# Modulation sums moved to the tensor engine, and the first expert's tokens chosen by rank

## The chip, the core and the metric

The kernel runs on one core of one Trainium2 chip. The metric is the device time of one execution in microseconds; shown is the median over runs. A profile is one further execution, recorded by the hardware profiler. All numbers in the model are float32.

## The reference, cut to what matters

The kernel computes a mixture-of-experts block followed by two layers of another block (feed-forward, mixer, feed-forward). Only the first block is touched by the change:

```python
SEQ = 256; D_MODEL = 1024; N_EXPERTS = 16; EC_CAPACITY_FACTOR = 2; D_FF_EXPERT = 2048

def expert_choice_moe(h, w_router, w_gate, w_up, w_down):
    cap = EC_CAPACITY_FACTOR * S // E                                  # 32 tokens
    affinity = jax.nn.softmax((h @ w_router).astype(jnp.float32), axis=-1)
    gates, idx = lax.top_k(jnp.swapaxes(affinity, 1, 2), cap)          # each expert picks its tokens
    xe = h[b_idx, flat_idx].reshape(B, E, cap, D)
    a = jnp.einsum('becd,edf->becf', xe, w_gate)
    u = jnp.einsum('becd,edf->becf', xe, w_up)
    ye = jnp.einsum('becf,efd->becd', jax.nn.silu(a) * u, w_down)
    ye = ye * gates[..., None].astype(ye.dtype)
    return jnp.zeros_like(h).at[b_idx, flat_idx].add(ye.reshape(B, E * cap, D).astype(h.dtype))

# first_block
mod = jax.nn.silu(c) @ w_ada[l] + b_ada[l]
shift_m, scale_m, gate_m, shift_f, scale_f, gate_f = [m[:, None, :] for m in jnp.split(mod, 6, axis=-1)]
h = rmsnorm(x, g_pre_mix[l]) * (1.0 + scale_m) + shift_m
proj = h @ w_in[l]
...                                       # retention and dilated attention, y_ret and y_att
mixed = jnp.concatenate([y_ret, y_att], axis=-1) @ w_out[l]
x = x + gate_m * rmsnorm(mixed, g_post_mix[l])
h = rmsnorm(x, g_pre_ffn[l]) * (1.0 + scale_f) + shift_f
moe = expert_choice_moe(h, w_router[l], w_gate_e[l], w_up_e[l], w_down_e[l])
x = x + gate_f * rmsnorm(moe, g_post_ffn[l])
```

The six modulations are numbered j = 0 to 5 below. The three weight matrices of one expert have 8 MiB each; the sixteen experts together have 384 MiB.

## The kernel before, in words

Tokens lie on the partitions in two tiles of 128 (t = 0, 1); the model width of 1024 is cut into eight pieces of 128 (k). Large products are made from a rounded high part and a remainder: `pieces` splits a weight on ScalarE (high) and on VectorE or GpSimd (remainder), and `mm3` (L115 to L117) does three matmuls.

The first block is the function `first`. Modulations 0 and 1 are computed at once: `mod_bank` (L253) multiplies a weight by `cb`, the vector silu(c) copied 32 times, so that each matmul fills 32 of the 128 PSUM rows (L260). Then a loop of 16 steps runs: `chan` computes 128 columns of the in-projection (24 matmuls of 128x258; its small side products are L474), then `mod_step(i)` does a part of modulations 2 to 5, then a piece of attention or retention. On every second step `mod_step` loads 512 rows of `w_ada` (2 MiB, `ada` and `block`), and on each step `mod_unit` adds two rows of eight into an accumulator `macc` on VectorE (L308 for the first, L310 for the rest, 128x1024 each). A modulation that is ready is summed over the partitions on TensorE, with `macc` as the weights (`mod_sum_cols`, L316) or a matrix of ones (`mod_sum_rows`, L329).

Behind the loop stand the out-projection (`mmo`), the residual (`to_x`, L348 and L350, with the tile `yg`, whose upper half is `gm`), the router's logits (transposes L728, copies L730 and L732, matmuls L735, softmax L737 to L741), and the choice of tokens: the affinities are transposed (L742), four rounds of max and replace find 32 tokens for each of the 16 experts (L780, L781), a running sum gives each its place (L782 to L785), and the places become one-hot matrices `sall` (L797). The tokens of expert 0 are gathered with `xh` and `xl`, the high and low parts of the scaled `x` (L806 and L807, four matmuls for each of the eight pieces k), into `x0`; the others' are gathered into `xe` between the two down blocks of expert 0.

`experts` (L872) goes through the experts in order. Each has two blocks of gate and up weights (4 MiB each, matmuls L898), then silu, a product (L911), four transposes, and two blocks of down weights (L943). A block of 4 MiB lies in a tile of the pool `ringx`, which has three (`xblock`, L91). Expert 0 also uses tiles left free by the stages before: four of `ring` for its second gate block (`unit`, L65), and nine `wx` tiles for its first down block (`extra`, L706).

All weight loads are issued by SyncE's queue, one after the other. A load waits there until the last reader of its tile is done, and everything behind it in the queue waits too. Instructions on each engine run in the order of the program as a list scheduler writes it.

Of the kernel before, what the change touches and what calls it, by code (L numbers as in the profile page):

```python
# [15 lines left out]
P = 128  # L16
# [19 lines left out]
class K:  # L36
# [3 lines left out]
    def __init__(s, ctx, tc):  # L40
# [5 lines left out]
        s.nblock = s.npiece = 0  # L46
# [167 lines left out]
    def consts(s):  # L214
# [13 lines left out]
        V.tensor_tensor(s.dist, s.r1, s.r2, OP.add)  # L228
        n = s.tmp()
# [68 lines left out]
    def mod_row(s, I, i, acc, eng):  # L298

        s.nc.gpsimd.memset(acc, 0.0)  # L300
        eng.dma_start(acc[0:1, :], I["b_ada"][0:1, i * D:(i + 1) * D])
# [10 lines left out]
    def mod_sum_cols(s, i, acc):  # L312

        pt = s.bank("acc", (KT, 2))
        for k in range(KT):
            s.nc.tensor.matmul(pt[:, k, :], s.quads(acc, k), s.one[:, :2], start=True, stop=True)  # L316
        mc = s.sm.tile([P, 2, 4], F32, tag="mc", name="mc", bufs=4)
        s.nc.vector.tensor_tensor(mc, s.fcol[:, 2 + 2 * i:4 + 2 * i, :], pt.rearrange("p (q r) o -> p q r o", r=4)[:, :, :, 0], OP.add)
        return mc
# [5 lines left out]
    def mod_sum_rows(s, acc, out):  # L325

        for n in range(2):
            pt = s.bank("acc")
            s.nc.tensor.matmul(pt, s.one, acc[:, half(n)], start=True, stop=True)  # L329
# [33 lines left out]
    def first(s, I, mid):  # L363
# [21 lines left out]
        V.memset(one, 1.0)  # L385

# [75 lines left out]
        shb = sm.tile([P, KT, 32], F32, name="shb", bufs=1, tag="cb")  # L462
# [140 lines left out]
        def mod_step(i):  # L603
            j, u = 2 + i // 4, i % 4
            if u == 0:
                accm[j] = t4("av", (D,)) if j == 5 else pa.tile([P, D], F32, tag="xn", name="macc", bufs=2)
                if j == 2:
                    s.mod_row(I, j, accm[j], A)
            if u % 2 == 0:
                accm["w"] = s.ada(I, j, u // 2)  # L610
            s.mod_unit(accm["w"][u % 2], u, accm[j], j > 2)
# [80 lines left out]
        ex0 = []  # L692

        def next_dma(d):

            if s.last0:
                s.queue(d, s.last0)
            s.last0 = d

        s.last0 = None  # L700

        def extra(*tiles):
            for pool, tag, m, n in tiles:
                u = pool.tile([P, m], F32, tag=tag, name="wx", bufs=n)
                o = sum(i.shape[1] for i in ex0)
                s.udma = nc.sync.dma_start(u, s.rows_x(I, "w_down_e", 0, 0)[:, o:o + m])  # L706
                next_dma(s.udma)
                ex0.append(u)

        t1 = lambda tag: (pa, tag, 1024, 1)  # L710
        extra(*[t1(i) for i in ("aq", "ak", "rqk", "rv")])
# [5 lines left out]
        pa_t = s.bank("tr")  # L717
# [5 lines left out]
        def logits(t):  # L723
# [18 lines left out]
            T.transpose(pa_t[:ne, tok(t)], aff[:, t, :], s.ident)  # L742
# [6 lines left out]
        s.ringx = s.c1.enter_context(s.tc.tile_pool(name="ringx", bufs=3, reuse_waits="tile"))  # L749
        w0 = {}  # L750
        for b in range(2):
            for n in ("w_gate_e", "w_up_e"):
                v = s.rows_x(I, n, 0, b)
                if b and n == "w_gate_e":
# [821 lines left out]
```

## Time and profile before

| what | us |
|---|---|
| median of three runs (2278.76 to 2280.75) | 2280.57 |
| the profiled execution's own time | 2279.83 |
| its span in the profile | 2278.1 |
| PE busy in the span | 1869.2 |
| VectorE busy in the span | 984.5 |
| ScalarE busy in the span | 730.3 |

The program has four parts on the time line: the start and the in-projection loop to about 153 us, the out-projection and the router to about 199 us, the sixteen experts to about 1111 us, and the second block behind them. PE is the tensor engine, PEld its weight loads, DVE VectorE, ACT ScalarE, POOL GpSimd, SP SyncE; an engine's name with a q is its queue of DMA issues. A matmul of float32 appears as two instructions in the trace, so counts there are twice those in the code. A matmul's time in the trace runs to its modelled end, so that neighbours overlap: the distance between two starts is what each costs. PEclk is the granted share of the tensor engine's full clock, 2.4 GHz; at 0.5 it runs at 1.2 GHz.

### The profile page before, as it was taken

The page shows a single profiled execution, that of the slowest core. Times are in us where ns is not written, and L with a number is a line of the kernel's source. Part 1 is how long each engine was busy: PE and PEld are TensorE (multiplying, and loading weights), DVE is VectorE, ACT ScalarE, POOL GpSimd, SP SyncE. Part 2 cuts the span into 40 slices and gives each one's busy share as a digit, 9 for nine tenths or more (in the row PEclk, how much of TensorE's full clock was granted, in tenths as well). Part 3 has the DMA queues.
Part 4 walks back from the last instruction along what each step waited for, and adds up shares of the span by engine and source line. Part 5 has one row for each costly group of instructions (what it writes and reads, how often), then busy time and mean ns, then how long its engine had stood idle before and what let it go on. Part 6 is the DMA issues. An engine that isn't in the chain of part 4 may idle for free.

```text
span 2278.1 us, 29561 instructions
## 1 busy us (share of the span) xinstructions
PE 1869.2 (82%) x12453; PEld 1352.3 (59%) x12453; DVE 984.5 (43%) x1577; ACT 730.3 (32%) x1205; POOL 157.1 (7%) x164
## 2 busy tenths in 40 slices
PE   7898765565555566556699999999999999999998
PEld 5685211111111111111399989899999998989997
DVE  6984200000000010000365568965556556896554
ACT  4542000000000000000254456854435445685443
POOL 2321000000000000000100032200000003200000
PEclk9997888878788778888799999999999999999999
DMA  8857999999999999999865545546546555544651
GB/s 329 328 222 329 435 432 429 430 429 432 429 429 431 432 429 431 431 432 430 311 231 182 199 166 181 181 157 222 186 156 222 181 198 166 176 171 164 220 185 56
DMA packets 190547, 659.58 MB, mean 290 GB/s; under 512 B 6867, under 2 KB 144331, under 8 KB 177486
## 3 DMA queue, kind: packets, MB, share of 16 engines
q1 hardware_dynamic: 189452, 657.06, 74.1%
q8 instruction: 97, 1.59, 0.3%
q10 hardware_dynamic: 962, 0.64, 0.1%
q14 instruction: 36, 0.29, 0.0%
HBM read 656.62 MB, written 1.05 MB: 289 GB/s over the span
## 4 chain that ended last, share of the span: by engine, by line
PE 59%; DMA 30%; DVE 5%; ACT 2%; POOL 2%; issue 1%; ACTq 0%; SPq 0%; POOLq 0%; DVEq 0%
DMA w<-in_w_down_e_dram 15%; DMA w<-in_w_gate_e_dram 14%; PE up L115 8%; PE up L117 8%; PE up L116 8%; PE acc L116 6%; PE acc L117 6%; PE acc L115 5%; PE acc L898 4%; PE up L943 4%; PE up L150 4%; PE up L154 2%; POOL uc L1255 1%; DVE v L1286 1%; DMA w<-in_w_up_e_dram 1%
## 5 line engine op out<-in xcount | busy, mean ns | idle before, releaser
L102 DVE TENSOR_TENSOR hl<-w,hl 128x1024 fp32r<-128x1024 f32 x376 | 458.0, 1230 | 253.7 <-ACT hl L101 253.5
L101 ACT ACTIVATE hl<-w 128x1024 fp32r<-128x1024 f32 x388 | 404.8, 1057 | 271.6 <-PE up L117 106.4
L115 PE MATMUL up<-hTh,hl 128*128 128x256 f32 x1664 | 470.2, 283 | 1.1 <-ACT uc L1276 1.1
L116 PE MATMUL up<-hTl,hl 128*128 128x256 f32 x1664 | 467.4, 281 | 0.0
L117 PE MATMUL up<-hTh,hl 128*128 128x256 f32 x1664 | 467.4, 281 | 0.0
L115 PEld LDWEIGHTS up<-hTh,hl 128*128 128x128 f32 x1664 | 313.3, 188 | 4.1 <-ACT uc L1276 1.9
L116 PEld LDWEIGHTS up<-hTl,hl 128*128 128x128 f32 x1664 | 313.6, 188 | 1.9
L117 PEld LDWEIGHTS up<-hTh,hl 128*128 128x128 f32 x1664 | 313.5, 188 | 0.0
L943 PE MATMUL up<-w,tmp 128*32 128x512 f32 x992 | 155.1, 777 | 104.7 <-DMA w<-in_w_down_e_dram 104.2
L900 ACT ACTIVATE tmp<-acc 128x512 f32<-128x512 f32 x16 | 9.6, 597 | 700.3 <-PE acc L898 700.3
L911 DVE TENSOR_TENSOR tmp<-tmp,acc 128x512 f32<-128x512 f32 x16 | 11.0, 688 | 514.7 <-PE acc L898 514.7
L115 PE MATMUL acc<-hl,a 128*128 128x512 f32 x528 | 209.9, 398 | 0.0
L116 PE MATMUL acc<-hl,a 128*128 128x512 f32 x528 | 208.6, 395 | 0.0
L117 PE MATMUL acc<-hl,e 128*128 128x512 f32 x528 | 208.6, 395 | 0.0
L898 PE MATMUL acc<-w,rqk 128*32 128x512 f32 x480 | 96.3, 944 | 126.7 <-DMA w<-in_w_up_e_dram 66.3
L943 PEld LDWEIGHTS up<-w,tmp 128*32 128x32 f32 x992 | 38.7, 137 | 209.4 <-issue 112.9
L898 PE MATMUL acc<-w,aq 128*32 128x512 f32 x480 | 80.7, 806 | 75.7 <-DMA w<-in_w_up_e_dram 75.4
L898 PEld LDWEIGHTS acc<-w,rqk 128*32 128x32 f32 x480 | 16.2, 138 | 184.7 <-DMA w<-in_w_up_e_dram 80.4
L948 DVE COPY pr<-up 128x512 f32<-128x512 f32 x16 | 11.1, 691 | 251.0 <-PE up L943 251.0
L117 PEld LDWEIGHTS acc<-hl,e 128*128 128x128 f32 x528 | 98.9, 187 | 24.4 <-DVE e L984 0.2
L115 PEld LDWEIGHTS acc<-hl,a 128*128 128x128 f32 x528 | 99.1, 188 | 21.5
L116 PEld LDWEIGHTS acc<-hl,a 128*128 128x128 f32 x528 | 99.1, 188 | 21.3
(370 smaller groups left out, 2327.5 us busy)
## 6 DMA issues: line engine op xcount, KB each, us to landing
w<-in_w_up_e_dram SPq DMA_DIRECT2D x32, 4096.0 KB, 25.3
w<-in_w_gate_e_dram SPq DMA_DIRECT2D x31, 4096.0 KB, 23.3
w<-in_w_down_e_dram SPq DMA_DIRECT2D x30, 4096.0 KB, 23.9
w<-in_ffn_w_up_dram SPq DMA_DIRECT2D x88, 1024.0 KB, 5.6
w<-in_ffn_w_down_dram SPq DMA_DIRECT2D x44, 1024.0 KB, 5.0
w<-in_w_in_dram SPq DMA_DIRECT2D x42, 1024.0 KB, 5.7
w<-in_w_ada_dram SPq DMA_DIRECT2D x8, 2048.0 KB
w<-in_w_out_dram SPq DMA_DIRECT2D x12, 1024.0 KB, 6.9
```

The costliest lines, as they stand in the source:

```text
L101: a = s.nc.scalar.activation(t[:, 0], src, AF.Copy)
L102: b = (eng or s.nc.vector).tensor_tensor(t[:, 1], src, t[:, 0].bitcast(F32), OP.subtract)
L115: a = mm(out, st[0], mv[0], start=start, stop=False)
L116: mm(out, st[0], mv[1], start=False, stop=False)
L117: s.mm = mm(out, st[1], mv[0], start=False, stop=stop)
L150: a = mm(out, h[0][:, k, tok(t)], ws[k // 4][i][:, k % 4, :], start=k + i == 0, stop=False)
L154: s.mm = mm(out, h[1][:, k, tok(t)], ws[k // 4][0][:, k % 4, :], start=False, stop=k == KT - 1)
L898: T.matmul(gu[i][32 * g:32 * g + 32, :], xk, col, start=k == 0, stop=k == KT - 1)
L943: T.matmul(dn[r:r + 32, :], ht[:, j % 4, 32 * g:32 * g + 32], w[2 * j + n], start=b == 0 and j < 2, stop=b == 1 and j > 5)
L948: V.tensor_copy(pr, dn)
L1255: G.tensor_tensor(nx[:, lo:], cur[:, lo:], cur[:, lo - sh:16 + S - sh], OP.add)
L1286: V.scalar_tensor_tensor(v, c[:, 13 + k:13 + k + S], self.cw[:, k, hd:hd + 1], v, OP.mult, OP.add)
```

## The change

The sums of modulations 2 to 5 are made on TensorE. `mod_half` multiplies four rows of eight by `cb`, as `mod_bank` does, at every second step of the loop; its PSUM bank is then copied or added into a tile of 128x512. Only one row in 32 of that tile is used further: `mod_sum_cols` transposes it, and `mod_sum_rows` picks its rows with the matrix `sel`.

```diff
-    def mod_unit(s, w, u, acc, first):
-        for a in range(2):
-            c = s.sc[:, 2 * u + a:2 * u + a + 1]
-            if first and u + a == 0:
-                s.nc.vector.tensor_scalar(acc, w[:, a, :], c, None, OP.mult)
-            else:
-                s.nc.vector.scalar_tensor_tensor(acc, w[:, a, :], c, acc, OP.mult, OP.add)
+    def mod_half(s, w, u, m, bias=None):
+        pt = s.bank("up")
+        for a in range(4):
+            for n in range(2):
+                r = 32 * (2 * (a % 2) + n)
+                s.nc.tensor.matmul(pt[r:r + 32, :], s.cb[:, 4 * u + a, :], w[a // 2][:, a % 2, half(n)], start=a < 2, stop=a > 1)
+        if u:
+            V.tensor_tensor(m, pt, m, OP.add)
+        elif bias is not None:
+            V.tensor_tensor(m, pt, bias, OP.add)
+        else:
+            V.tensor_copy(m, pt)
...
         def mod_step(i):
...
+            if i % 2 == 0:
+                accm["w"] = s.ada(I, j, u)
+            else:
+                s.mod_half(accm["w"], u, accm[j], bias2 if j == 2 else None)
```

The tokens of expert 0 are found without the top-k rounds. Each token's affinity to expert 0 is spread along a row by a matmul, and three comparisons for each half of the tokens count, in their accumulator output, how many tokens stand ahead of it (equal ones that come earlier count too). The count is the token's rank, and a comparison with 0 to 31 gives the one-hot matrix `sl0`, scaled by the token's norm. The gather multiplies `x` itself in float32. The choice for all experts (`choose`, the rounds as before) is issued behind the second half of that gather, and the one-hot matrices and `xh`, `xl` (`spread`) behind the transposes of expert 0's product; the gathers of the others stand behind both down blocks.

```diff
+        for t in range(2):
+            T.matmul(bc[:, tok(t)], aff[:, t, 0:1].to_broadcast([P, P]), s.ident, start=True, stop=True)
...
+            V.scalar_tensor_tensor(jk(0), bc[:, tok(t)], a0, s.early, OP.is_equal, OP.mult, accum_out=cnt[:, t, 0:1])
+            for i in range(2):
+                V.scalar_tensor_tensor(jk(1 + i), bc[:, tok(i)], a0, one, OP.is_ge if t > i else OP.is_gt, OP.mult, accum_out=cnt[:, t, 1 + i:2 + i])
+        V.tensor_tensor(rank, cnt[:, :, 0], cnt[:, :, 1], OP.add)
+        V.scalar_tensor_tensor(rank, rank, 1.0, cnt[:, :, 2], OP.add, OP.add)
+        for t in range(2):
+            V.tensor_scalar(sl0[:, t], iof[:, 0], rank[:, t:t + 1], y2[t], OP.is_equal, OP.mult)
...
         def gather0(k):
-            gather(k, 1, s.bank("tr")[:, :32], x0[:, k, :])
+            pt = s.bank("tr")[:, :32]
+            for t in range(2):
+                T.matmul(pt, s.quads(x[:, t, :], k), sl0[:, t], start=t == 0, stop=t == 1)
+            A.activation(x0[:, k, :], pt, AF.Identity, scale=af[:, k:k + 1], bias=bf[:, k:k + 1])
```

Expert 0's weights lie in more tiles, and are loaded in another order. `ringx` has two tiles and a new pool `ringy` one; the `wx` tiles now take its second up block and the first half of its second down block.

```diff
-        extra(*[t1(i) for i in ("aq", "ak", "rqk", "rv")])
+        up1 = extra(rows0("w_up_e", 1), 4096, *[t1(i) for i in ("aq", "ak", "rqk")])
...
+        for n in ("w_gate_e", "w_up_e"):
+            w0[n, 0] = s.xblock(rows0(n, 0))
+            next_dma()
+        up1 += extra(rows0("w_up_e", 1), 7168, t1("rv"))
+        for j in range(0, 8192, 2048):
+            us.append(s.unit(v[:, j:j + 2048]))
+            next_dma()
+        dn1 = extra(rows0("w_down_e", 1), 0, t1("ya"))
+        w0["w_up_e", 1] = extra(rows0("w_up_e", 1), 0, (pd, "hh", 2048, 1), (pd, "hl", 2048, 1)) + up1
+        w0["w_down_e", 0] = s.xblock(rows0("w_down_e", 0))
+        next_dma()
+        dn1 += extra(rows0("w_down_e", 1), 1024, xn2, xn2, tmp2, tmp2)
```

On VectorE, in the loop of the in-projection, the rows before are these (`sme`, `mx` and `tmp` belong to attention, `hl` are remainders of split weights):

```order
L515 RECIPROCAL sme_630<-sme_630 128x2
L310 SCALAR_TENSOR_TENSOR macc_682<-w_789,sc_106,macc_682 128x1024
L517 TENSOR_SCALAR tmp_624<-tmp_624,sme_630 128x256 x2
L515 RECIPROCAL sme_642<-sme_642 128x2
L508 SCALAR_TENSOR_TENSOR tmp_731<-acc_725,tmp_731 128x512
L517 TENSOR_SCALAR tmp_636<-tmp_636,sme_642 128x256 x2
L511 TENSOR_REDUCE mx_735<-tmp_731 128x2
L508 SCALAR_TENSOR_TENSOR tmp_743<-acc_726,tmp_743 128x512
L310 SCALAR_TENSOR_TENSOR macc_682<-w_789,sc_106,macc_682 128x1024
```

and the rows now, at the same place:

```order
L532 RECIPROCAL sme_642<-sme_642 128x2
L534 TENSOR_SCALAR tmp_636<-tmp_636,sme_642 128x256 x2
L532 RECIPROCAL sme_654<-sme_654 128x2
L534 TENSOR_SCALAR tmp_648<-tmp_648,sme_654 128x256 x2
L298 TENSOR_TENSOR hl_787<-w_252,hl_787 128x512
L298 TENSOR_TENSOR hl_824<-w_252,hl_824 128x512
L313 TENSOR_TENSOR m_694<-up_731,bias2_118 128x512
L525 SCALAR_TENSOR_TENSOR tmp_747<-acc_741,tmp_747 128x512
L525 SCALAR_TENSOR_TENSOR tmp_759<-acc_742,tmp_759 128x512
L528 TENSOR_REDUCE mx_751<-tmp_747 128x2
L528 TENSOR_REDUCE mx_763<-tmp_759 128x2
```

Two additions of 128x1024 into `macc` stood between attention's steps; they are gone, and one row of 128x512 out of the bank `up`, into `m`, stands for four of them.

On SP, up to expert 1's first up block, the queue before is this, from the load of `w_out` on (128x8192 is a block of 4 MiB, 128x1024 one of half a MiB):

```order
L65 DMA w<-in_w_out_dram 128x2x1024 x4
L706 DMA wx<-in_w_down_e_dram 128x1024 x4
L91 DMA w<-in_w_gate_e_dram 128x8192
L91 DMA w<-in_w_up_e_dram 128x8192
L65 DMA w<-in_w_gate_e_dram 128x2048 x4
L91 DMA w<-in_w_up_e_dram 128x8192
L706 DMA wx<-in_w_down_e_dram 128x1024 x3
L91 DMA w<-in_w_down_e_dram 128x8192
L706 DMA wx<-in_w_down_e_dram 128x512 x2
L91 DMA w<-in_w_gate_e_dram 128x8192
L91 DMA w<-in_w_up_e_dram 128x8192
```

and now, from expert 0's first gate block on:

```order
L92 DMA w<-in_w_gate_e_dram 128x8192
L92 DMA w<-in_w_up_e_dram 128x8192
L722 DMA wx<-in_w_up_e_dram 128x1024
L65 DMA w<-in_w_gate_e_dram 128x2048 x4
L722 DMA wx<-in_w_down_e_dram 128x1024
L722 DMA wx<-in_w_up_e_dram 128x2048 x2
L92 DMA w<-in_w_down_e_dram 128x8192
L722 DMA wx<-in_w_down_e_dram 128x1024 x2
L722 DMA wx<-in_w_down_e_dram 128x512 x2
L92 DMA w<-in_w_down_e_dram 128x4096
L92 DMA w<-in_w_gate_e_dram 128x8192
L92 DMA w<-in_w_up_e_dram 128x8192
```

Expert 0's first up block no longer lies where `yg` lay, its first down block has moved ahead of the small pieces of the second, and expert 1's blocks follow behind all of expert 0's.

On PE, from the logits on, the rows before are these (the pair L806 and L807 is the gather for one piece of 128; two such pairs, one for each token tile, make one k):

```order
L728 MATMUL acc_1845<-ident_64,x_89 128x128 x4
L728 MATMUL acc_1851<-ident_64,x_89 128x128 x4
L735 MATMUL up_1857<-awr_1471,tmp_1843 128x16 x4
L735 MATMUL up_1857<-awr_1471,tmp_1844 128x16 x4
L728 MATMUL acc_1887<-ident_64,x_89 128x128 x4
L728 MATMUL acc_1893<-ident_64,x_89 128x128 x4
L735 MATMUL up_1899<-awr_1471,tmp_1885 128x16 x4
L735 MATMUL up_1899<-awr_1471,tmp_1886 128x16 x4
L742 MATMUL tr_1762<-ident_64,aff_1759 16x128 x2
L788 MATMUL tr_1957<-ident_64,tmp_1954 128x16 x2
L806 MATMUL tr_1971<-sall_1961,xhh_1927 128x32
L807 MATMUL tr_1971<-sall_1961,xhl_1928 128x32
```

and now:

```order
L746 MATMUL acc_1913<-ident_64,x_89 128x128 x4
L746 MATMUL acc_1919<-ident_64,x_89 128x128 x4
L746 MATMUL acc_1954<-ident_64,x_89 128x128 x4
L746 MATMUL acc_1960<-ident_64,x_89 128x128 x4
L753 MATMUL up_1925<-awr_1517,tmp_1911 128x16 x4
L753 MATMUL up_1925<-awr_1517,tmp_1912 128x16 x4
L753 MATMUL up_1966<-awr_1517,tmp_1952 128x16 x4
L753 MATMUL up_1966<-awr_1517,tmp_1953 128x16 x4
L789 MATMUL tr_1993<-ident_64,aff_1809 128x128 x2
L816 MATMUL tr_2018<-sl0_1999,x_89 128x32
L816 MATMUL tr_2022<-sl0_1999,x_89 128x32
```

The transposes of both token tiles now stand ahead of the logits of both, the two transposes of the affinities and of the places are gone from there, and two matmuls that spread the affinities of expert 0 have come in.

## Rows read from the trace of the kernel before

**Rows 1.** Windows: start and end, busy by engine (instructions), PEclk, DMA share, GB/s.

```profile
64.00:104.00 40.00, 33.81 (x228) 26.90 (x226) 38.34 (x65) 26.09 (x73) 17.21 (x11) 0.95 0.84 323
104.00:153.00 49.00, 49.00 (x336) 45.74 (x336) 41.70 (x70) 21.18 (x50) 7.55 (x5) 0.90 0.61 230
165.00:182.00 17.00, 16.63 (x80) 13.15 (x78) 11.77 (x24) 9.16 (x20) 4.29 (x5) 1.00 0.01 2
190.00:205.00 15.00, 7.03 (x31) 4.87 (x35) 9.55 (x25) 5.81 (x9) 7.03 (x6) 0.50 1.06 448
270.00:1110.00 840.00, 501.78 (x3000) 131.67 (x2992) 68.96 (x147) 24.32 (x47) 0.11 (x1) 0.82 1.00 429
```

**Rows 2.** Chain of waits, 250 to 280 us: start, length, what.

```profile
253.54 15.72 DMA w<-in_w_up_e_dram
```

**Rows 3.** Chain of waits, 1080 to 1115 us.

```profile
1086.28 24.41 DMA w<-in_w_down_e_dram
1110.74 1.98 PE up L943 x8
```

**Rows 4.** Time line of SP's issues: start, length, line, what.

```profile
153.91 0.33 SPq L91 DMA_DIRECT2D w<-in_w_gate_e_dram  x1
182.12 0.33 SPq L91 DMA_DIRECT2D w<-in_w_up_e_dram  x1
...
229.04 0.33 SPq L91 DMA_DIRECT2D w<-in_w_up_e_dram  x1
```

**Rows 5.** Chain of waits, 58 to 104 us: shares by line.

```profile
by line: DVE macc L310 16.6%; DVE tmp L517 15.9%; issue 12.1%; DVE tmp L508 9.3%; PE tr L474 8.1%; DVE mx L511 8.1%; DVE hl L294 7.9%; POOL tmp L506 5.1%; ACT tmp L514 4.5%; PE acc L535 1.9%; PE up L115 1.6%; PE up L117 1.5%; PE up L116 1.5
```

**Rows 6.** Chain of waits, 104 to 153 us: shares by line.

```profile
by line: PE up L115 21.6%; PE up L117 21.0%; PE up L116 20.2%; PE acc L316 15.2%; PE acc L566 7.3%; PE acc L535 6.3%; PE acc L549 4.3%; PE tr L526 2.7%; PE tr L558 1.8%
```

**Rows 7.** Chain of waits, 50 to 153 us.

```profile
52.14 3.62 PE up L260 x32
...
58.26 1.86 PE tr L474 x32
60.13 0.32 PE up L116
...
141.28 3.62 PE acc L316 x16
```

**Rows 8.** Time line of PE, 145 to 153 us.

```profile
145.78 0.42 PE L116 MATMUL up<-hl 128*128 128x258 f32 x1
...
147.06 0.42 PE L116 MATMUL up<-hl 128*128 128x258 f32 x1
...
151.16 0.29 PE L115 MATMUL up<-hh,hl 128*128 128x258 f32 x1
...
151.89 0.29 PE L115 MATMUL up<-hh,hl 128*128 128x258 f32 x1
```

**Rows 9.** Chain of waits, 180 to 240 us: router, choice and expert 0.

```profile
182.99 1.05 PE up L735 x8
...
185.51 3.59 PE up L735 x16
...
190.52 0.40 PE tr L742
...
198.61 0.38 PE tr L806
...
202.81 5.18 PE acc L898 x32
...
225.41 3.62 PE acc L898 x32
229.11 0.70 DVE tmp L911
...
231.41 3.56 PE up L943 x28
```

**Rows 10.** Time line of ScalarE at the end of the softmax.

```profile
189.81 0.19 ACT L739 ACTIVATION_READ_ACCUMULATOR aff<-lt,mx 128x1 f32 x1
```

More of the change, by code (lines that the diff above doesn't have):

```diff
@@ L323, in quads, with mod_sum_rows @@
         return ap.rearrange("p (q c r) -> p q r c", r=4, c=P)[:, k // 4, k % 4, :]
-    def mod_sum_rows(s, acc, out):
+    def mod_sum_rows(s, m, out):
         for n in range(2):
             pt = s.bank("acc")
-            s.nc.tensor.matmul(pt, s.one, acc[:, half(n)], start=True, stop=True)
+            s.nc.tensor.matmul(pt, s.sel[:, n, :], m, start=True, stop=True)
             s.nc.vector.tensor_tensor(out[:, half(n)], pt, out[:, half(n)], OP.mult)
@@ L779, in first @@
[L779 to L789 removed]
+        bc = s.bank("tr")[:, :S]
@@ L815, in gathers @@
                 xe.extend(t4(n, (2, 512)) for n in ("aq", "ak", "rqk", "rv"))
-            gather(k, ne, s.bank("acc"), xe[k // 2][:, k % 2, :])
+            pt = s.bank("acc")
+            for t in range(2):
+                sl = sall[:, t].rearrange("p e c -> p (e c)")
+                for i in range(2):
+                    T.matmul(pt, s.quads(xs[i][:, t, :], k), sl, start=t + i == 0, stop=t + i == 2)
+            V.tensor_scalar(xe[k // 2][:, k % 2, :], pt, af[:, k:k + 1], bf[:, k:k + 1], OP.mult, OP.add)
         def later():
@@ L829, in later @@
                 pt = s.bank("tr")
-                T.matmul(pt, one, accm[5][:, half(n)], start=True, stop=False)
+                T.matmul(pt, s.sel[:, n, :], accm[5], start=True, stop=False)
                 T.matmul(pt, one[0:1, :], row[0:1, half(n)], start=False, stop=True)
@@ L835, in first_expert @@
         def first_expert(w, b):
-            if w == "w_down_e" and b == 0:
-                extra(t1("ya"), *[(pa, "xn", 1024, 2)] * 2, *[(pd, "tmp", 512, 6)] * 2)
-                return [u[:, i:i + 512] for u in ex0 for i in range(0, u.shape[1], 512)]
-            return w0[w, b] if (w, b) in w0 else s.xblock(s.rows_x(I, w, 0, b))
-        ye = s.experts(I, x0, xe, gts, gather0, gathers, later, mid, first_expert)
+            if (w, b) in w0:
+                return w0[w, b]
+            return dn1 + s.xblock(rows0(w, b)[:, 4096:])
+        ye = s.experts(I, x0, xe, gts, gts0, gather0, gathers, choose, spread, later, mid, first_expert)
         yx = s.cp.tile([P, 2], F32, name="yx")
@@ L870, in rows_x, with experts @@
         return I[w][0, e, n * b:n * b + n, :].rearrange("(p r) f -> p (r f)", p=P)
-    def experts(s, I, x0, xe, gts, gather0, gathers, later, mid, first_expert):
+    def experts(s, I, x0, xe, gts, gts0, gather0, gathers, choose, spread, later, mid, first_expert):
         nc = s.nc
@@ L918, in experts @@
             A.activation(ht, pt, AF.Copy)
+            if e == 0:
+                spread()
             if e == NE - 1:
@@ L942, in experts @@
                         r = 64 * n + 32 * (j % 2)
-                        T.matmul(dn[r:r + 32, :], ht[:, j % 4, 32 * g:32 * g + 32], w[2 * j + n], start=b == 0 and j < 2, stop=b == 1 and j > 5)
-                if e + b == 0:
-                    for k in range(KT):
-                        gathers(k)
+                        T.matmul(dn[r:r + 32, :], ht[:, j % 4, 32 * g:32 * g + 32], u[2 * j + n], start=b == 0 and j < 2, stop=b == 1 and j > 5)
+            if e == 0:
+                for k in range(KT):
+                    gathers(k)
             pr = pa.tile([P, 512], F32, tag="xn", name="pr", bufs=2)
```

186 lines of the change are left out of this document (95 added, 91 removed).

## The prediction

> **What bounds the kernel.** I read the windows by stage first, then the chain of waits inside the stages, then SP's time line. Between 270 and 1110 us the DMA share is 1.00 at 429 GB/s [rows 1], and the chain there runs through the landings of weight blocks, with 24.41 us of waiting for one and then 1.98 us of PE [rows 3]. So the experts take as long as their bytes. Behind the last landing, 1110.74 [rows 3], the change touches nothing but the operand of two matmuls, and I carry that part over at its old length. A microsecond is therefore won only where the DMA stands still before the experts' stream closes up: its share is 0.61 between 104 and 153 us and 0.01 between 165 and 182 [rows 1]. SP's time line says why: expert 0's first gate block is issued at 153.91, and the next issue, its first up block, comes at 182.12, held behind the last reader of `yg`, where it lies [rows 4].
>
> The yardstick is the landing of expert 1's first up block, since all blocks behind it follow back to back. Its second up block lands at 253.54 + 15.72 = 269.26 [rows 2], the last down block at 1110.74 [rows 3]. Between them lie 86 blocks of 4 MiB (96 in all, ten landed by then): 841.5 / 86 = 9.78 us each. Two blocks earlier, the first up block landed at 269.3 - 19.6 = 249.7. What the changed kernel gains is 249.7 less the new landing.
>
> **The new order of loads.** All of expert 0 is now queued ahead of expert 1, and most of it lies where the in-projection or nothing lay. From the split of the last in-projection chunk on, about 149 us, 28 MiB up to expert 1's first gate block flow at 9.78 per 4 MiB, 68.5 us, less some 2 us for pieces that go earlier: DMA runs dry at 215 to 218. The next load, expert 1's first up block, takes the tile of expert 0's first down block, so it is issued when PE has read that. Call that time R. A lone 4 MiB block takes at most 165 - 153.9 = 11.1 us, as the DMA is idle from 165 on [rows 1, 4]. The new landing is R + 11.1, and R is what has to be worked out.
>
> **Modulation sums.** In 64 to 104 us VectorE is busy for 38.34 of 40 us [rows 1], and the chain of 58 to 104 runs through it; the sums L310 alone hold 16.6% of its 46 us, 7.6 us [rows 5], and go. In 104 to 153 PE is busy throughout [rows 1]; L316 holds 15.2% of 49 us, 7.4 us [rows 6], and becomes eight transposes of 0.40 / 2 each [rows 9], 1.6: 5.8 go. Added are eight half sums on PE. Sixteen such matmuls, 32 instructions, take 3.62 us [rows 7], so a half sum costs 1.81. Four in the second stretch cost 7.2 in full. Four in the first cost between 1.0, if they fill PE's 40 - 33.81 = 6.2 idle us, and 7.2. At worst the loop is 7.2 + 7.2 - 7.6 - 5.8 = 1.0 us longer; at best 5.2 shorter, and 4.9 more if the clock of 0.90 in the second stretch [rows 1] becomes full. I take 4.5 shorter, range -1 to 10. VectorE's eight reads of the bank are 0.70 each, the price of a 128x512 row [rows 9], 5.6 us in place of some 36; they lie beside PE.
>
> Here the Trainium skill speaks against the change. First the row: at a switch in the trace, from matmuls with 32 weight columns (L474) to one with 128 (L116), the start follows the end without a gap, 58.26 + 1.86 = 60.12 against 60.13 [rows 7]. The Trainium skill's page TensorEngine Tiling (Array Packing), section Key Properties, says that changing the tiling mode drains the engine. By that rule each of 16 switches would add about the overhang of a matmul (0.42 of length less 0.21 of distance, [rows 8]), 3.4 us in all, and the gain would be so much smaller. The trace does not show it, and I take nothing for the switches.
>
> **Logits and choice.** Before, the first gather starts at 198.61 [rows 9]. It moves by three things. The loop gives 4.5. The logits matmuls of token tile 0 now stand behind the transposes of tile 1 and ahead of tile 1's logits: two groups of 1.05 [rows 9], 2.1, or 3.59 at the clock of that moment, less the 0.7 us that they can start before tile 1's copies are done: 1.4 to 2.9, I take 2.2 later. The affinities are final at 190.5, where their transposes L742 begin, so transposes, top-k, scan and one-hot take 198.61 - 190.52 = 8.1 [rows 9]. The rank puts in their place two matmuls, 0.40 [rows 9]; six comparisons of 128x128, which lie between the 0.19 of a row with one column [rows 10] and the 0.70 of 512 [rows 9], by columns 0.32, 1.9 together; two tiny sums of 0.2 and two one-hot rows a little above, 0.25. That is 3.2. The six accumulator outputs are not in the trace for VectorE; ScalarE's read of one is that row of 0.19, so they add 0 to 1.1. I take 3.7, range 2.9 to 4.6. First gather: 198.61 - 4.5 + 2.2 - (8.1 - 3.7) = 191.9, range 184 to 199.
>
> **Expert 0.** The gather in float32 is 16 matmuls with 128x128 weights; L316 is eight such in 3.62 us [rows 7], so 7.2. Gate and up are 128 instructions: 3.62 for 32, or 5.18 [rows 9] in the stretch with a granted clock of 0.50 [rows 1], so 14.5 to 20.7; I take 16.5, a clock that rises on the way. From their end, 225.41 + 3.62, to the down block at 231.41 [rows 9] it was 2.4 us; four small transposes, 0.8, now stand in it. The scalings of `spread` on ScalarE and VectorE wait for tiles that the second up block frees half way, so they lie beside its last matmuls; were they late, they would put two rows of 0.70 ahead of the product. The top-k rounds, some 7 us, lie beside the gate and up matmuls. The first down block is 32 instructions, 3.56 x 32 / 28 = 4.1. Sum 7.2 + 16.5 + 3.2 + 4.1 = 31.0, range 29 to 35. R = 191.9 + 31.0 = 222.9, so the block lands at 234.0, 15.7 us earlier than 249.7. The idle DMA between 216 and 223 is what is given back. The gathers of the other experts, now in one piece, are 32 matmuls of at most the 0.38 of one before [rows 9], 12 us. They end by 239, and expert 1's first gate matmuls by 243, when the block that is then being loaded, expert 1's second gate block, lands (234.0 + 9.8); so its next load can follow without a gap, and they add nothing.
>
> The profiled execution was 2279.83 us long, 0.7 below the median; I subtract from the median: 2280.57 - 15.7 = 2265.
>
> **Rivals.**
> - A, the forecast: R between 218 and 228, 2260 to 2270. For it: each term has a row. 0.50.
> - B, no gap: the clock comes back in the loop and in expert 0, R is before 217, the DMA never idles and expert 1's block lands 9.8 after it at 225 to 227, 23 to 25 us earlier: 2257. For it: the clock was 0.90 in the loop's second stretch [rows 1], and L316 goes. Against: it takes 10 us from the loop. 0.13.
> - C, the loop gains nothing, because PE was its limit or because each switch of weight width costs 0.2 us there, and expert 0's gate and up run at half clock, 4 us longer: R = 228 to 234, 2270 to 2276. For it: PE busy 49.00 of 49 [rows 1]; against the switches: no gap at the one above. 0.24, of which 0.05 for the switches. Their rule is the Trainium skill's, from the page named above.
> - D, no change: R at 234 to 243 because several of these fall together. 0.06.
> - E, slower: the clock falls to half in the loop. Where L316 ended, the matmuls L116 stood (147.06 - 145.78) / 2 = 0.64 apart, against 0.73 / 2 = 0.37 for L115 at full clock [rows 8]; a chunk of 24 then takes 5.1 in place of 2.9 us, 2.2 more. If the short half sums and VectorE's reads of their bank between chunks did that to PE, R would be later than 243 from some ten of sixteen chunks on; for all of them 35 us later, R = 258, landing 269, so 2300. Against it: the 32 instructions of the same kind before the loop took 3.62 [rows 7], the better of the two prices that gate matmuls of the same size have. 0.07.
>
> **How the numbers follow.** The time is A's. A alone spans 2260 to 2270; with B and most of C the range is 2257 to 2276. A measurement of this kernel tells 0.2%, 4.6 us, from no change. A, B and C lie below 2276: faster 0.87; D 0.06; E 0.07.
>
> **What would show it.** In the new profile expert 0's gate and up blocks should be issued together near 149 us, and DMA be busy from there; a gap of about 7 us should stand ahead of the issue of expert 1's first up block near 223. The first gather should start near 192, the last in-projection matmul near 148.5, and the last block land near 1095. The prediction is wrong if that last landing moves by less than 5 us, if the loop's end does not move, or if the length behind the last landing changes.

## The result, and the profile after

The changed kernel takes 2264.71 us (median of 2262.14 to 2267.83), the kernel before 2280.24 on the same chip; the ratio is 0.9934, with a 95% interval of 0.9916 to 0.9951. That is 15.5 us less, and 2265 was forecast. The profiled execution of the changed kernel is the longest of its four, 2267.83 us, with a span of 2266.1; against the 2279.83 of the kernel before it is 12.0 us shorter. In a second set (the run e8 below) the profiled execution is again the longest, 2267.70 of 2261.71 to 2267.70. So the traces show a gain of 12, and some 3.5 us more stand in executions that were not traced.

The windows of the changed kernel (columns as in [rows 1]):

```profile
64.00:104.00 40.00, 40.00 (x322) 30.75 (x318) 28.09 (x57) 26.48 (x76) 10.76 (x8) 1.00 0.94 361
104.00:146.00 42.00, 42.00 (x349) 33.76 (x344) 21.84 (x60) 19.49 (x47) 7.33 (x7) 1.00 0.54 211
165.00:182.00 17.00, 14.52 (x69) 12.80 (x67) 9.00 (x27) 6.33 (x18) 2.93 (x4) 0.73 1.01 419
195.00:205.00 10.00, 10.00 (x65) 2.72 (x57) 0.00 (x0) 0.23 (x1) 0.00 (x0) 0.74 0.71 257
216.00:226.00 10.00, 8.73 (x78) 2.98 (x74) 5.86 (x9) 3.93 (x7) 2.06 (x2) 1.00 0.13 54
270.00:1095.00 825.00, 503.50 (x2946) 129.28 (x2946) 67.02 (x143) 23.46 (x45) 0.11 (x1) 0.79 1.00 430
```

VectorE has fallen from 38.34 to 28.09 busy us of 40 between 64 and 104, and PE is now busy throughout at a full granted clock, where it had 0.95 and 0.90 [rows 1]. The DMA, at 0.01 between 165 and 182 before, now runs at 1.01. In its place it stands at 0.71 around 200 us and at 0.13 between 216 and 226. The experts' stream itself has the rate it had.

SP's time line, its issues of 4 MiB and one of 2 MiB (128x4096, at 201.11):

```profile
146.58 0.33 SPq L92 DMA_DIRECT2D w<-in_w_gate_e_dram  x1
146.95 0.56 SPq L92 DMA_DIRECT2D w<-in_w_up_e_dram  x1
...
201.11 0.33 SPq L92 DMA_DIRECT2D w<-in_w_down_e_dram  x1
204.55 0.33 SPq L92 DMA_DIRECT2D w<-in_w_gate_e_dram  x1
225.47 0.33 SPq L92 DMA_DIRECT2D w<-in_w_up_e_dram  x1
```

Expert 0's gate and up blocks go out together at 146.6, where the up block had waited until 182.12 [rows 4]. Expert 1's first up block goes out at 225.47, when expert 0's first down block has been read: that is R, and the gap ahead of it is the 0.13 above. The chain of waits behind it:

```profile
240.31 17.99 DMA w<-in_w_up_e_dram
```

```profile
1074.18 24.45 DMA w<-in_w_down_e_dram
```

Expert 1's second up block lands at 258.30, 11.0 earlier than the 269.26 of [rows 2]; the last block at 1098.63, 12.1 earlier than 1110.74 [rows 3]. From there to the end it is 1169.1 and 1169.2 us (2279.83 - 1110.74 and 2267.83 - 1098.63). All but 1.1 us was won ahead of that second up block, as forecast.

How the steps came out in the profiled execution:

| step | forecast | measured |
|---|---|---|
| loop, its end | -4.5 | 153.70 to 146.48, -7.2 |
| out-projection and residual, until `x` of tile 1 | 0 | -2.9 more (184.61 to 174.50) |
| from `x` of tile 1 to the last affinity | +2.2 | 5.8 to 10.8, +5.0 |
| from there to the first gather | -4.4 | 8.1 to 3.4, -4.7 |
| first gather | 191.9 | 188.70 |
| from there to R | 31.0 | 36.8 |
| R | 222.9 | 225.47 |
| R to the landing of the up block | 11.1 | 13.2 (258.30 - 19.6 - 225.47) |

The time line of PE at the first half sum (L309; L118 is the last matmul of a chunk of the in-projection, L518 belongs to attention):

```profile
69.20 0.28 PE L118 MATMUL up<-hh,hl 128*128 128x258 f32 x1
69.41 1.92 PE L309 MATMUL up<-w,cb 128*32 128x512 f32 x16
71.27 1.14 PE L518 MATMUL acc<-ak,aq 64*128 64x256 f32 x8
```

The 16 instructions take 1.86 us from start to start (71.27 - 69.41). The first of them starts 0.21 behind the matmul ahead, where matmuls of a chunk stand 0.12 apart.

VectorE's time line at the router (L748 copies transposed tokens, L759 is the last step of the softmax, L799 the rank's first comparison):

```profile
174.42 0.68 DVE L748 COPY tmp<-acc 128x512 f32<-128x512 f32 x1
...
179.15 0.69 DVE L748 COPY tmp<-acc 128x512 f32<-128x512 f32 x1 [3.98 <-PE up L753]
...
185.11 0.23 DVE L759 TENSOR_SCALAR aff<-aff,sme 128x16 f32<-128x16 f32 x1
186.23 0.35 DVE L799 SCALAR_TENSOR_TENSOR tmp<-tr,aff,early 128x128 f32<-128x128 f32 x1 [0.89 <-PE tr L789]
186.51 0.08 DVE L799 DVE_READ_ACCUMULATOR tmp<-tr,aff,early 128x1 f32 x1
```

The copy for token tile 1 at 179.15 has waited 3.98 us for PE's L753, the logits of tile 0, which themselves stand behind both transposes. This is a part of the extra 5.0 of the table; e3 below takes it apart. The comparison takes 0.35, and the read of its accumulator 0.08; the next comparison starts 0.28 behind the first, so that reads cost nothing.

PE's chain in expert 0 (L816 gather, L945 gate and up, L989 down), and its time line at the first break:

```profile
188.70 2.04 PE tr L816 x8
...
191.90 1.85 PE acc L945 x2
...
194.81 9.67 PE acc L945 x62
...
207.56 1.85 PE acc L945 x2
...
210.48 8.72 PE acc L945 x62
...
221.83 7.00 PE up L989 x64
```

```profile
188.70 3.19 PE L816 MATMUL tr<-sl,x 128*128 128x32 f32 x12 [2.51 <-DVE sl L805]
191.82 1.92 PE L945 MATMUL acc<-w,x 128*32 128x512 f32 x2
```

The gate and up matmuls take 9.67 + 8.72 us for 62 instructions each, where 7.0 was the price at full clock (PEclk is 0.72 from 194.8 to 204.5 and 0.81 from 210.5 to 219.2), and in each half one matmul (two instructions) stands alone among the gather's and takes 1.85.

### The profile page after: what moved, and what is told of

It is laid out like the page before. It is cut to its first block, busy times and chain, and to the rows that moved or that the text cites. A ratio compares the mean times of both kernels' runs of the same rounds, so it can differ in the third digit from the quotient of the medians.

```text
span 2266.1 us, 29800 instructions
## 1 busy us (share of the span) xinstructions
PE 1882.0 (83%) x12561; PEld 1345.9 (59%) x12561; DVE 953.1 (42%) x1568; ACT 732.0 (32%) x1209; POOL 145.2 (6%) x165
## 3 DMA queue, kind: packets, MB, share of 16 engines
HBM read 656.62 MB, written 1.05 MB: 290 GB/s over the span
## 4 chain that ended last, share of the span: by engine, by line
PE 61%; DMA 30%; DVE 3%; POOL 2%; ACT 2%; issue 1%; SPq 0%; POOLq 0%; DVEq 0%; ACTq 0%
DMA w<-in_w_gate_e_dram 15%; DMA w<-in_w_down_e_dram 14%; PE up L116 8%; PE up L118 8%; PE up L117 8%; PE acc L117 6%; PE acc L116 6%; PE acc L118 6%; PE acc L945 5%; PE up L989 4%; PE up L151 4%; PE up L155 2%; POOL uc L1301 1%; DMA w<-in_w_up_e_dram 1%; DVE v L1332 1%
## 5 line engine op out<-in xcount | busy, mean ns | idle before, releaser
L116 PE MATMUL up<-hTh,hl 128*128 128x256 f32 x1664 | 470.2, 283 | 1.1 <-ACT uc L1322 1.1
L118 PE MATMUL up<-hTh,hl 128*128 128x256 f32 x1664 | 467.4, 281 | 0.0
L117 PE MATMUL up<-hTl,hl 128*128 128x256 f32 x1664 | 467.4, 281 | 0.0
L116 PEld LDWEIGHTS up<-hTh,hl 128*128 128x128 f32 x1664 | 313.3, 188 | 4.1 <-ACT uc L1322 1.9
L117 PEld LDWEIGHTS up<-hTl,hl 128*128 128x128 f32 x1664 | 313.6, 188 | 1.9
L118 PEld LDWEIGHTS up<-hTh,hl 128*128 128x128 f32 x1664 | 313.4, 188 | 0.0
L989 PE MATMUL up<-w,tmp 128*32 128x512 f32 x1008 | 155.0, 769 | 95.4 <-DMA w<-in_w_down_e_dram 95.4
L116 PE MATMUL acc<-hl,a 128*128 128x512 f32 x528 | 209.9, 397 | 0.0
L117 PE MATMUL acc<-hl,a 128*128 128x512 f32 x528 | 208.6, 395 | 0.0
L118 PE MATMUL acc<-hl,e 128*128 128x512 f32 x528 | 208.5, 395 | 0.0
L945 PE MATMUL acc<-w,rqk 128*32 128x512 f32 x480 | 100.5, 984 | 112.9 <-DMA w<-in_w_up_e_dram 62.7
L989 PEld LDWEIGHTS up<-w,tmp 128*32 128x32 f32 x1008 | 38.4, 136 | 200.9 <-issue 106.5
L945 PE MATMUL acc<-w,aq 128*32 128x512 f32 x480 | 81.8, 814 | 85.5 <-DMA w<-in_w_up_e_dram 85.3
L945 PEld LDWEIGHTS acc<-w,rqk 128*32 128x32 f32 x480 | 17.1, 151 | 178.2 <-DMA w<-in_w_up_e_dram 77.2
L118 PEld LDWEIGHTS acc<-hl,e 128*128 128x128 f32 x528 | 99.0, 187 | 24.3 <-DVE e L1030 0.2
L994 DVE COPY pr<-up 128x512 f32<-128x512 f32 x16 | 11.1, 692 | 241.5 <-PE up L989 241.5
L116 PEld LDWEIGHTS acc<-hl,a 128*128 128x128 f32 x528 | 99.2, 188 | 21.4
L117 PEld LDWEIGHTS acc<-hl,a 128*128 128x128 f32 x528 | 99.1, 188 | 21.3
```

The source lines that it names most:

```text
L116: a = mm(out, st[0], mv[0], start=start, stop=False)
L117: mm(out, st[0], mv[1], start=False, stop=False)
L118: s.mm = mm(out, st[1], mv[0], start=False, stop=stop)
L945: T.matmul(gu[i][32 * g:32 * g + 32, :], xk, col, start=k == 0, stop=k == KT - 1)
L989: T.matmul(dn[r:r + 32, :], ht[:, j % 4, 32 * g:32 * g + 32], u[2 * j + n], start=b == 0 and j < 2, stop=b == 1 and j > 5)
L994: V.tensor_copy(pr, dn)
```

## The experiments

All times are medians beside runs of the kernel before on the same chip, at 2280.0 to 2280.7 us. The changed kernel's own nine times lie between 2261.71 and 2267.83, so a gain of 3 us against its median, as in e3 and e10, is little more than this spread; e4, e5, e7 and e11 are clear of it.

| run | us | ratio to before, 95% interval |
|---|---|---|
| e1, sums only | 2269.99 | 0.9955 (0.9940 to 0.9970) |
| e2, rank and loads only | 2275.91 | 0.9981 (0.9972 to 0.9990) |
| e3, logits in turn | 2261.06 | 0.9920 (0.9904 to 0.9937) |
| e4, up block in the ring | 2257.94 | 0.9904 (0.9889 to 0.9918) |
| e5, e3 and e4 together | 2256.20 | 0.9898 (0.9883 to 0.9912) |
| e6, choice by top-k | 2270.67 | 0.9959 (0.9938 to 0.9980) |
| e7, half sums twice | 2278.17 | 0.9993 (0.9983 to 1.0002) |
| e8, the changed kernel again | 2264.33 | 0.9931 (0.9918 to 0.9943) |
| e9, choice by top-k again | 2270.97 | 0.9960 (0.9946 to 0.9973) |
| e10, gather unbroken | 2261.56 | 0.9913 (0.9896 to 0.9929) |
| e11, e3, e4 and e10 together | 2254.40 | 0.9884 (0.9869 to 0.9899) |

**e1 and e2: the change in two parts.** e1 takes `mod_half`, the two sums behind it and `sel` into the kernel before; e2 takes them out of the changed kernel.

```diff
+            if i % 2 == 0:
+                accm["w"] = s.ada(I, j, u)
+            else:
+                s.mod_half(accm["w"], u, accm[j], bias2 if j == 2 else None)
```

> The kernel before with the modulation sums on the tensor engine and nothing else of the change. Theory 1 (the sums carry the gain): the loop ends some 6 us earlier and the out-projection some 2 more, because its remainders no longer stand behind the sums on VectorE; the first up block, which waits for the residual's reader of yg, is issued near 173 instead of 182, and everything behind it moves with it: about 2271 us, 9 less than before. Rival (the load order carries it): the loop's gain is lost again since the order of loads is the old one: 2277 or more.

> The changed kernel with the modulation sums back on VectorE. Theory 1: the loop and the out-projection end where they did before; the rank saves about 4.7 us of choice, the logits behind both transposes cost about 4.5, expert 0 takes about 36 us from its first gather, so its first down block is read near 235 and expert 1's first up block lands near 248 instead of 249.7: 2279 us, within 2 of before. Rival (the load order carries the gain): 2270 or less.

e1 is 10.3 us faster than before, e2 4.4; their sum is 14.7, and the whole change gave 15.5. SP's time line and the chain of e1:

```profile
146.34 0.33 SPq L91 DMA_DIRECT2D w<-in_w_gate_e_dram  x1
172.21 0.33 SPq L91 DMA_DIRECT2D w<-in_w_up_e_dram  x1
```

```profile
243.56 15.51 DMA w<-in_w_up_e_dram
```

The first gate block goes out at 146.34 (before: 153.91 [rows 4]), the up block that waits for the reader of `yg` at 172.21 (before: 182.12): 9.9 earlier, 2.3 of it behind the loop. The second up block lands at 259.07, 10.2 earlier than [rows 2]. So the old order of loads passes the sums' gain on in full, and theory 1 holds. In e2 the gain was forecast at 1.3 and is 4.4:

```profile
154.54 0.33 SPq L92 DMA_DIRECT2D w<-in_w_gate_e_dram  x1
...
231.61 0.33 SPq L92 DMA_DIRECT2D w<-in_w_up_e_dram  x1
```

```profile
198.91 2.04 PE tr L804 x8
...
246.46 18.52 DMA w<-in_w_up_e_dram
```

Its loop ends 0.6 later than before (154.54) and its first gather, 198.91, starts 0.3 later; R is 32.7 behind that, not the 36 that I had taken from the changed kernel, whose gate and up matmuls met a lower clock. That is the 3 us of the miss. Of its two lone gate matmuls the first takes 1.85 again, the second 0.97, at a granted clock of 1.00:

```profile
216.28 0.97 PE acc L933 x2
```

**e3: logits in turn.** A dependence puts the transposes of tile 1 behind the last logits matmul of tile 0.

```diff
-                    T.transpose(pt[:, j, :], s.quads(x[:, t, :], 4 * hf + j), s.ident)
+                    a = T.transpose(pt[:, j, :], s.quads(x[:, t, :], 4 * hf + j), s.ident)
+                    if t and hf + j == 0:
+                        s.queue(a, s.log0)
...
+                s.log0 = T.matmul(pl, xT[k // 4][:, k % 4, :], awr[:, k, :], start=k == 0, stop=k == KT - 1)
```

> The changed kernel with the logits matmuls of token tile 0 ahead of the transposes of tile 1 on the tensor engine, as before the change. Theory 1 (the idle stretch of the DMA ends when expert 0's first down block is read, so a microsecond on the way there is one at the end): the first gather starts 3 to 4 us earlier than 188.7 and the read ends so much earlier than 225.5: 3 to 4 us less than the changed kernel. Rival (the way to that read is not what ends the idle stretch, or the weight-bound gather of expert 0 only waits elsewhere): within 1 us of the changed kernel.

```profile
185.70 2.04 PE tr L818 x8
...
234.21 17.70 DMA w<-in_w_up_e_dram
```

The first gather starts at 185.70, 3.0 earlier than in the changed kernel's trace (0.5 of it stood at the loop's end already), and the time falls by 3.7 (2261.06 against 2264.71). In the traces R moves by more, from 225.47 to 219.37, and the last landing with it, from 1098.63 to 1092.30, since expert 0's second half also met a full clock here (62 instructions in 7.03 in place of 8.72). So a microsecond ahead of R comes back at the end, while the DMA waits for R. That the copy had to wait at all may come from the two `tmp` tiles of six that now hold weights; the code suggests it, and no run took it apart.

The order on PE is only half of the extra 5.0: from `x` of tile 1 to the last affinity e3 still needs 8.3 us (174.04 to 182.37), where the kernel before needed 5.8. Most of the other half stands in VectorE's order. Before, its copy of tile 0's tokens ran ahead of the last step of tile 1's residual (L350 at 183.20); in the changed kernel and in e3 it runs behind that step (L358, at 172.63 in e3), and PE's logits of tile 0 wait for it. The lines are VectorE's before, and VectorE's and PE's in e3:

```profile
182.23 0.68 DVE L730 COPY tmp<-acc 128x512 f32<-128x512 f32 x1
```

```profile
173.96 0.68 DVE L750 COPY tmp<-acc 128x512 f32<-128x512 f32 x1
```

```profile
174.69 1.06 PE L755 MATMUL up<-awr,tmp 128*128 128x16 f32 x8 [2.26 <-DVE v L161]
```

The releaser named in the last row (`v`, L161) is the small step right behind the copy. No run moved this copy back.

**e4: expert 1's first up block in the ring's four tiles**, which expert 0's second gate block leaves early.

```diff
+            if e == 1 and w == "w_up_e" and b == 0:
+                v = s.rows_x(I, w, e, b)
+                us = [s.unit(v[:, j:j + 2048]) for j in range(0, 8192, 2048)]
+                return [u[:, i:i + 1024] for u in us for i in (0, 1024)]
```

> The changed kernel with expert 1's first up block loaded into the four tiles that held expert 0's second gate block, which are free some 10 us before the tile of its first down block. Theory 1 (the idle DMA from 216.6 to 225.5 is lost time): the load is issued in pieces near 214 to 216, the stretch closes, and the time falls by 8 to 10 us against the changed kernel, to about 2256. Rival (the tensor engine, late in expert 0, is then what holds the next loads): the gap moves to expert 1's second gate block and less than 3 us are won.

```profile
207.89 2.90 SPq L65 DMA_DIRECT2D w<-in_w_up_e_dram  x4
```

```profile
216.00:226.00 10.00, 9.92 (x69) 3.38 (x70) 3.04 (x5) 0.41 (x2) 2.05 (x2) 0.83 1.08 451
```

The block goes out in four pieces from 207.89 on, and the DMA share between 216 and 226 is 1.08 in place of 0.13. The time falls by 6.8 (2257.94 against 2264.71), in the traces by 10.5 (last landings 1088.13 and 1098.63), the traced execution of the changed kernel being the later one. The stretch was lost time, and R no longer decides. Expected were 8 to 10; the idle stretch of a median execution may be shorter than the traced one, but no trace of such an execution shows it.

**e5: e3 and e4 together.**

> The two edits of the runs before together: expert 1's first up block in the tiles of expert 0's second gate block, and the logits of token tile 0 ahead of the transposes of tile 1. Theory 1 (the first edit alone already leaves the DMA almost no idle time from 147 us on, so an earlier first gather has nothing to give back): within 1.5 us of the first edit alone, 2256.5 to 2258. Rival (the tensor engine's lateness in expert 0 still costs): both gains add, 2254.5 or less.

1.7 us less than e4, where theory 1 allowed 1.5, and 1.7 above the rival's 2254.5. The two sets of times overlap (2255.52 to 2258.79 and 2257.29 to 2259.45), so that the size is not settled; e3 had given 3.7 alone. The trace does not help: it is of the longest of the four executions, and its first gather is later than that of e4 (188.01 against 187.06).

**e6 and e9: the choice by top-k rounds ahead of expert 0's gather**, in the changed kernel.

```diff
+        choose()
+        pt0 = s.bank("tr")
+        for t in range(2):
+            T.transpose(pt0[:, t * ne:(t + 1) * ne], ces[0][:, t * P:(t + 1) * P], s.ident[:ne, :ne])
+        V.tensor_copy(rank, pt0[:, :2 * ne].rearrange("p (t e) -> p t e", t=2)[:, :, 0])
```

> The changed kernel with expert 0's tokens again from the top-k rounds, which stand ahead of its gather; sums, gather in float32 and loads as changed. Theory 1: the choice takes 8.1 us in place of 3.4 from the last affinity to the first gather, the read of expert 0's first down block comes 4.7 us later, and so does the end: about 2269.5. Rival (the rank is hidden, because expert 0's matmuls wait for weights): within 1 us of the changed kernel.

> The choice by top-k rounds once more: in its first run the profiled execution moved its weights at 403 and 414 GB/s for some 400 us where the others hold 430, which hid the term. Theory 1: the read of expert 0's first down block comes 3.5 to 4.7 us later than in the changed kernel, and the undisturbed times are so much longer, 2268 to 2270. Rival (the choice was hidden): the same as the changed kernel within 1 us.

The times of e6 run from 2263.36 to 2287.79, those of e9 from 2266.70 to 2286.70, far wider than any other kernel's. Both traced executions are the longest of their sets. Time lines of VectorE (last affinity) and PE (first gather) in e9, and its windows:

```profile
184.83 0.23 DVE L759 TENSOR_SCALAR aff<-aff,sme 128x16 f32<-128x16 f32 x1
```

```profile
191.86 3.22 PE L799 MATMUL tr<-sl,x 128*128 128x32 f32 x12 [0.59 <-DVE sl L824]
```

```profile
300.00:500.00 200.00, 123.70 (x716) 32.07 (x708) 13.99 (x27) 5.87 (x12) 0.00 (x0) 0.79 1.00 432
500.00:700.00 200.00, 114.42 (x678) 29.79 (x682) 12.94 (x24) 4.40 (x9) 0.00 (x0) 0.80 1.01 419
700.00:900.00 200.00, 113.46 (x668) 29.09 (x660) 21.35 (x59) 7.19 (x12) 0.00 (x0) 0.80 1.00 398
```

From the last affinity to the first gather it is 6.8 us, so the rank saves 3.4 (the scan and the comparison with -1 are quicker here than in the kernel before, 0.68 and 0.28 us against 1.63 and 0.89, with less GpSimd work beside them; not tested). R is at 227.25, 2.3 behind that of e8. But the DMA moves 419 and 398 GB/s between 500 and 900 us at a share of 1.00, in both traces of this kernel, which costs some 20 us and lies in a stretch that the edit does not touch; why it does is open. The times do not decide between theory 1 and its rival: five of e9's six lie at 2266.70 to 2271.83, about 6 above e8's 2264.33, but four of e6's ten lie at 2263.36 to 2265.42, where the changed kernel is, and how much of any of them the slower stream holds is not known. That the rank is worth its 3.4 us at the end is therefore argued from the traces, not shown by times.

**e7: each half sum issued twice.**

```diff
+        for rep in range(2):
+            for a in range(4):
```

> The changed kernel with the eight matmuls of each half sum issued twice into the same bank (the second set starts afresh, so the result is the same). It adds 8 x 1.85 = 14.8 us to the tensor engine in the loop. Theory 1 (the loop is now bound by the tensor engine and everything behind it moves with its end): 14 to 15 us more than the changed kernel, about 2279.5, that is as slow as the kernel before. Rival (the loop still waits for VectorE or loads in places, which hides part): 5 to 10 us more.

```profile
160.59 0.34 SPq L92 DMA_DIRECT2D w<-in_w_gate_e_dram  x1
...
237.47 0.33 SPq L92 DMA_DIRECT2D w<-in_w_up_e_dram  x1
```

14.8 us of matmuls make the loop's end 14.0 later (160.59 against 146.58) and the time 13.5 longer. The loop is bound by PE now, nearly to the last microsecond, and what is added in it arrives at the end.

**e8: the changed kernel again.**

> The changed kernel once more, beside the next run on one chip, since both spread over several microseconds. Theory 1 (the spread comes from the tensor engine's clock in expert 0, which moves the read of expert 0's first down block): times between 2262 and 2268, and the profiled read moves with them, about 222 where the time is 2264.5.

2264.33, from 2261.71 to 2267.70. Its trace is of the longest time again, with R at 224.98. So the theory of the spread could not be tried on a short execution; it stays open. In its favour: the 62 gate and up instructions of expert 0's second half take 8.72 and 8.80 in the two traces of this kernel, and 7.03 in those of e2, e3, e4, e5 and e7.

**e10: the gather in one piece**, by a dependence of the first gate matmul and the first up matmul of each half on the half's last gather.

```diff
+                            if e + r + g == 0:
+                                s.queue(a, s.g0)
```

> The changed kernel with each half of expert 0's gather kept in one piece: in the changed kernel the scheduler put one gate matmul of 32 columns among the gather's matmuls in each half, and it stands there for 1.85 us. Theory 1 (such a matmul alone takes as long as the four of a group that fill the four column strips together, and what it costs comes before the read of expert 0's first down block): the two halves are 1.85 us shorter each less the 0.3 that the matmul costs in its group, so the read and the end come about 3 us earlier: 2261.5. Rival (the matmul fills a wait of the gather for its PSUM bank): the gather waits instead, less than 1 us.

```profile
187.99 4.12 PE L816 MATMUL tr<-sl,x 128*128 128x32 f32 x16 [2.50 <-DVE sl L805]
192.04 9.43 PE L945 MATMUL acc<-w,x 128*32 128x512 f32 x64
...
208.84 3.62 PE L945 MATMUL acc<-wx,x 128*32 128x512 f32 x32
```

```profile
218.77 0.33 SPq L92 DMA_DIRECT2D w<-in_w_up_e_dram  x1
```

The first half's gather takes 4.05 us in one piece, where from 188.70 to 194.81 it was 6.1 with the break, and the time falls by 3.2 (2261.56 against 2264.71), as theory 1 had it. The gather did not wait elsewhere, so the rival is out. R moves by more than that in the trace, 225.47 to 218.77, since the second half also met a full clock: 3.62 for 32. How much of the 3.2 is the lone matmuls and how much the clock is not taken apart.

**e11: e3, e4 and e10 together.**

> Expert 1's first up block in the ring's tiles, logits in turn and the gather unbroken, together. Theory 1 (the DMA is without long gaps since the first of them, but for a stretch of 10 us near 200 us at a share of 0.82, where the second down block waits for the read of the first gate block): some 1 to 2 us less than with the first two edits, 2254 to 2256. Rival (nothing left to give back): 2256 to 2257.

```profile
195.00:205.00 10.00, 10.00 (x78) 5.53 (x74) 2.18 (x7) 1.65 (x5) 0.00 (x0) 1.00 1.01 415
216.00:226.00 10.00, 10.00 (x77) 5.07 (x70) 3.96 (x6) 0.24 (x1) 1.95 (x2) 1.00 1.05 438
```

2254.40 us, the fastest version: 1.8 below e5, as theory 1 said (the two sets just touch, 2254.10 to 2255.68 and 2255.52 to 2258.79), with the DMA share at 1.01 and 1.05 in the two stretches that were open in the changed kernel. It is 10.3 below the changed kernel and 26.2 below the 2280.65 of the kernel before beside it. Against e4 the two further edits give 3.5, about half of the 3.7 and 3.2 that they gave alone.

## Why the prediction was right, point by point

**What bounds the kernel**: right. The stream of the experts and all behind it kept their lengths to about 1 us, and R decided: e3, e7 and e10 moved the way to R by some microseconds and the end moved with it, e4 freed the load from R and won the idle stretch.

**The mechanism of the loads**: right, including the idle stretch ahead of expert 1's first up block: some 7 us were forecast, and in the trace the share is 0.13 over 10 us, 8.7 idle. Not foreseen was a second one at 195 to 205, share 0.71, where the second down block's rest waits for the read of expert 0's first gate block (201.11).

**Modulation sums**: the sign and the bound were right (e7), the size was not: -7.2 in the loop, and 2.9 more behind it, against -4.5. I took 4.5 between -1 and 10 because I gave only part of the clock; it rose to 1.00 in both stretches. No run parts what the clock gave from what VectorE gave. (The row of 0.40 in [rows 9] is one transposition, not the two that I took it for; four together take 0.75 in the loop, L322 at 117.43, so that the 1.6 of the sum holds.) The -2.9 I had put at nothing. In the kernel before, PE waited twice in the out-projection, 1.25 us here and 0.62 at 162.28, for a weight's remainder (L294) on VectorE:

```profile
158.61 0.50 PE L116 MATMUL acc<-hl,yhh 128*128 128x512 f32 x1 [1.25 <-DVE hl L294]
```

Those remainders stood there behind the normalisation of the last retention piece, and this behind the last two sums (L310, at 150.76 and 152.60) and a step on GpSimd. Its step `q` (L580) ran at 156.73, behind the loop's end; in the changed kernel the same step runs at 144.23 (L597), ahead of it, and PE does not wait. e1 shows the gain alone (9.9 at the issue of the up block, 7.6 at the gate block). The chain of waits had those pieces in it, and I read only its loop.

**The switches of weight width**: nothing, as taken. A half sum costs 1.86 with its switches, against 1.81 from [rows 7]. The rows give 0.1 or less for each switch, and the same 0.1 stands where the width stays 128 (behind L583, 141.47 to 141.67). From the rule of a drain that the Trainium skill states (TensorEngine Tiling (Array Packing), Key Properties) I had estimated 3.4 us for the loop, which this trace does not show. My reading of the row before was too quick: pieces of a chain always join, and PE's time line at that place has L116 and L117 0.22 apart (60.06 and 60.28), 0.1 more than usual.

**Logits**: the step failed in size, 5.0 against 2.2. I priced the order on PE, and e3's trace gives 2.5 for it (10.8 to 8.3). I did not price that VectorE's copy of tile 0 falls behind the residual of tile 1, which stands for most of the rest.

**Choice**: the rank takes 3.4 where 3.7 was taken. It saves 4.7 against the rounds of the kernel before and 3.4 against those of e9. The accumulator reads that I put at 0 to 1.1 are 0.08 long and hidden under the next comparison. The Trainium skill's page VectorE: DVE Perf Modes, Two Vector instructions with no wait between them, says that such an operation is two instructions; the trace shows the second one.

**Expert 0**: the step failed, 36.8 against 31.0, beyond my bound of 35. The step that was mis-sized is gate and up, 22.1 against 16.5 (9.67 + 8.72 + 2 x 1.85); the gather took 1 us more than its 7.2. Two things were missing: the lone matmuls, 1.85 each, and that in this trace both halves, not only the first, run below full clock (9.67 and 8.72 for 62 instructions, 7.0 at full clock). Where the gather is unbroken and the second half has its clock, in e10, the step takes 30.8 (187.99 to 218.77), as forecast; with the lone matmuls and a full clock in the second half it is 32.7 in e2 and 33.7 in e3.

**The sum**: the errors are of both signs: -2.7, -2.9, +2.8, -0.3, +5.8 and +2.1 for the landing, 4.8 late in the traced execution, whose gain is 12.0 for 15.7 forecast. Why the landing took 13.2 and not 11.1 is open. The median's 15.5 agrees more closely than the steps deserve, and in part that is luck; it belongs to executions in which, as far as the times tell, R came earlier. Of the rivals, A's condition (R from 218 to 228) is what happened, B's clock came back in the loop but not in expert 0, and of C's half clock in expert 0 a part came true (0.72 and 0.81 in its two halves), while the loop gained.

## What to carry to other kernels

Where a stream of loads bounds a stage, work out when its buffers come free at its start, and price only what lies ahead of the last such release: a microsecond counts in full there (e3, e7, e10) and only in part once the release is moved to another buffer (e4, then e5 and e11). When an edit takes work off an engine, follow the queue behind the work too, as 2.3 to 2.9 us of the sums' gain lay behind the loop (e1, and the whole change). When a scheduler sets one narrow matmul among others, look at what that one costs alone.

## What the runs showed of the hardware

One gate matmul of 32 columns among matmuls of 128 takes 1.85 us in the changed kernel at the clock of 0.50 around it, and 0.97 in e2 at 1.00; eight of the half sum's matmuls, which fill four strips, take 1.86 together at full clock. In these kernels narrow matmuls were cheap only in company. On VectorE the accumulator's read took 0.08 us and did not delay the next comparison. And a kernel that differs only in the choice ran its weight stream at 398 to 419 GB/s between 500 and 900 us, in both of its profiled executions, where all others hold 430 or 431.
